# Loading and spreading V of the last two batches by halves in a tree-attention kernel

## The chip, the cores and the metric

The kernel runs on one core of one Trainium2 chip. The metric is device time in microseconds (us). A run is called fast or slow by its state: slow means over 1.5% above the fastest of the same kernel. Of the profile I use the span, from the first to the last instruction; a run's time is 1.7 to 1.9 us over its span. PE is the tensor engine. Its granted clock is in the profile too: 1.0 is full speed, and I call a stretch at 0.5 a half clock.

## The reference

Attention with a mask: query i sees key i and its ancestors in a binary tree.

```python
batch, heads, seq, dim = 8, 12, 512, 64
mask[i, i] = 1
while parent > 0: parent = (parent - 1) // 2; mask[i, parent] = 1
scores = einsum('bhqd,bhkd->bhqk', Q, K) / sqrt(dim) + (1 - mask) * (-1e9)
weights = exp(scores - max) / (sum + 1e-10)
out = einsum('bhqk,bhkd->bhqd', weights, V)
```

## The kernel before

The 96 heads are 48 pairs. GpSimd issues all loads, as float32 cast to bfloat16, in the order of `plan`; at most eight are in flight, as each later issue waits for the landing of the eighth load before it. Outputs leave through SyncE. The parts that matter are the order of the loads, the copies that spread V into the layouts v1 and vx (ten per spread, on the vector engine), and the loop.

```python
for b in range(1, B):                      # (at, tensor, batch, first head, last head + 1)
    at = HP * b - 2
    plan += [(at, Q, b, 0, 4), (at, K, b, 0, 4),
             (at + 2, Q, b, 4, 8), (at + 2, K, b, 4, 8)]
    if b < B - 1:
        plan += [(at + 3, V, b + 1, 0, H), (at + 4, Q, b, 8, H), (at + 4, K, b, 8, H)]
    else:
        plan += [(at + 4, Q, b, 8, 10), (at + 4, K, b, 8, 10),
                 (at + 5, Q, b, 10, H), (at + 5, K, b, 10, H)]
# ... cut ...
for i in range(N):                         # N = 48 pairs, HP = 6 pairs a batch
    b, hp = pairs[i]
    load(i + 9)
    if i + 2 < N:
        transposes(i + 2)                  # PE, then qt (vector engine) and kt (scalar engine)
    if i + 1 < N:
        scores(i + 1)                      # PE, then two exp on the scalar engine
    values(i)                              # PE, then rec and of on the vector engine, output DMA
    # ... cut: batch 0 ...
    elif b + 1 < B and hp:
        if hp == 1:
            todo = spread(b + 1, 0, H)     # ten copies, for all 12 heads
        copies(todo[2 * hp - 2:2 * hp])    # two in each of five steps
```

All PSUM tiles, which take what PE puts out, have one buffer.

The softmax here doesn't subtract the row's maximum and nothing guards it: scores larger than these inputs give would overflow.

Of the kernel before, what the change touches and what calls it, by code (L numbers as in the profile page):

```python
# [126 lines left out]
def kernel(  # L127
# [8 lines left out]
    B, H, S, D = Q.shape  # L136
# [3 lines left out]
    HP = H // 2  # L140
# [11 lines left out]
    for t in range(T):  # L152
        o = sorted(range(T), key=lambda r: KCOL[t, r])
        at = [KCOL[t, r] for r in o]
# [32 lines left out]
    for i in range(NV):  # L187
# [9 lines left out]
    psumO = ctx.enter_context(tc.tile_pool(name="psumO", bufs=1, space=PSUM))  # L197


    plan = [(0, Q, 0, 0, 2), (0, K, 0, 0, 2), (0, V, 0, 0, 6), (0, Q, 0, 2, 6),  # L200
            (0, K, 0, 2, 6), (0, V, 0, 6, H), (1, Q, 0, 6, 10), (1, K, 0, 6, 10),
            (3, Q, 0, 10, H), (3, K, 0, 10, H), (3, V, 1, 0, H)]
    for b in range(1, B):
        at = HP * b - 2
        plan += [(at, Q, b, 0, 4), (at, K, b, 0, 4),
                 (at + 2, Q, b, 4, 8), (at + 2, K, b, 4, 8)]
        if b < B - 1:
            plan += [(at + 3, V, b + 1, 0, H), (at + 4, Q, b, 8, H),
                     (at + 4, K, b, 8, H)]
        else:  # L210
            plan += [(at + 4, Q, b, 8, 10), (at + 4, K, b, 8, 10),
                     (at + 5, Q, b, 10, H), (at + 5, K, b, 10, H)]
    plan.reverse()
    loaded = {}

    def load(upto):
        while plan and plan[-1][0] <= upto:
            _, src, b, h0, h1 = plan.pop()
            kind = "q" if src is Q else "k" if src is K else "v"
            if (kind, b) not in loaded:  # L220
                loaded[kind, b] = stage.tile([P, H, T * D], bf16, name=kind + "s")
            nc.gpsimd.dma_start(  # L222
                out=loaded[kind, b][:, h0:h1, :],
                in_=src[b, h0:h1].rearrange("h (p t) d -> p h (t d)", t=T),
            )

    def pick(v, t0, t1):

        stop = t1 + (1 if t1 > t0 else -1)
        return v[:, :, t0:stop if stop >= 0 else None:t1 - t0, :]  # L230

    def spread(b, h0, h1):
        vs = loaded["v", b]
        v1, vx = v1s[b % NV], vxs[b % NV]
        v = vs[:, h0:h1, :].rearrange("p h (t d) -> p h t d", t=T)
        big = [
            (vx[64:P, h0:h1, 0:3:2, 0:D], v[64:P, :, 0:3:2, :]),
            (vx[0:64, h0:h1, 1:4:2, 0:D], v[64:P, :, 1:4:2, :]),
        ]
        for part, c, t0, t1 in ((0, 0, 1, 2), (32, 0, 3, 0), (64, 1, 2, 1),  # L240
                                (96, 1, 0, 3)):
            assert KORD[XW[c] + part // 32] == (t0, 1)
            assert KORD[XW[c + 2] + part // 32] == (t1, 1)
            big.append((
                vx[part:part + 32, h0:h1, c:c + 3:2, 0:D],
                pick(v[32:64], t0, t1),
            ))
        small = [
            (v1[32 * r:32 * r + 32, h0:h1, 0:D], v[0:32, :, KORD[K1 + r][0], :])
            for r in range(T)  # L250
        ]
        ops = []
        for n in range(6):
            ops.append(big[n])
            if n % 3:
                ops.append(small.pop())
        return ops

    def copies(ops):
        for o, i in ops:  # L260
            nc.vector.tensor_copy(out=o, in_=i)  # L261

    pairs = [(b, hp) for b in range(B) for hp in range(HP)]
    N = len(pairs)
    state = {}

    def transposes(i):
        b, hp = pairs[i]
        qs, ks = loaded["q", b], loaded["k", b]
        tq = psumT.tile([P, 512], bf16)  # L270
        tk = psumT.tile([P, 576], bf16)

        def put(o, src, t, mat):
            for hi in range(2):
                nc.tensor.matmul(  # L275
                    out=o[D * hi:D * hi + D], rhs=perms[mat],
                    lhsT=src[:, 2 * hp + hi, D * t:D * t + D],
                    start=True, stop=True, is_transpose=True,
                )

        put(tq[:, 64:192], qs, 0, 1)
        put(tq[:, 0:384].rearrange("d (c x) -> d c x", c=2)[:, :, 0:64], qs, 1, 0)
        for t in range(2, T):
            put(tq[:, P * t:P * t + P], qs, t, 0)
        for t in range(T):
            at = kput[t][1]
            if at[1] - at[0] == 32:
                step, run = at[2] - at[0], 64
            else:
                step, run = at[1] - at[0], 32  # L290
                assert at[2] - at[1] == step
            o = tk[:, at[0]:]
            o = bass.AP(o.tensor, o.offset, [list(o.ap[0]), [step, P // run], [1, run]])
            put(o, ks, t, 2 + t)
        qt = work.tile([P, 512], bf16)
        kt = work.tile([P, 512], bf16)
        nc.vector.tensor_copy(out=qt[:, :], in_=tq[:, :])  # L297
        nc.scalar.copy(  # L298
            out=kt[:, :].rearrange("d (i j x) -> d i j x", j=2, x=32),
            in_=tk[:, :].rearrange("d (j i x) -> d i j x", j=2, x=32)[:, 0:8],  # L300
        )
        state[i] = (qt, kt)
# [39 lines left out]
    def values(i):  # L342
        b, hp = pairs[i]
        v1, vx = v1s[b % NV], vxs[b % NV]
        et1, etx = state.pop(i)
        o2 = psumO.tile([P, 2, 512], fp32)
        for hi, order in ((0, (0, 1)), (1, (0, 1)), (0, (2, 3)), (1, (2, 3))):
            h = 2 * hp + hi
            for t in order:
                for kind in range(2):  # L350
                    parts = ((0, P, t),) if t >= 2 else (
                        (0, 64, 1 - t), (64, P, t))
                    for p0, p1, c in parts:
                        if kind == 0:
                            e, v = et1[:, hi, P * c + p0:P * c + p1], v1[:, h, 0:D + 1]
                        else:
                            e, v = etx[:, hi, c, p0:p1], vx[:, h, c, 0:D + 1]
                        nc.tensor.matmul(  # L358
                            out=o2[p0:p1, hi, (D + 1) * t:(D + 1) * (t + 1)],
                            lhsT=e, rhs=v, start=kind == 0, stop=kind == 1,  # L360
                        )
        o4 = o2[:, :, 0:T * (D + 1)].rearrange("p h (t x) -> p h t x", t=T)
        rec = opool.tile([P, 2, T, 1], fp32)
        nc.vector.reciprocal(out=rec[:, :, :, :], in_=o4[:, :, :, D:D + 1])  # L364
        of = opool.tile([P, 2, T * D], fp32)
        of4 = of[:, :, :].rearrange("p h (t d) -> p h t d", t=T)
        nc.vector.tensor_tensor(  # L367
            out=of4, in0=o4[:, :, :, 0:D],
            in1=rec[:, :, :, :].to_broadcast([P, 2, T, D]), op=ALU.mult,
        )  # L370
        nc.sync.dma_start(
            out=out[b, 2 * hp:2 * hp + 2].rearrange(
                "h (p t) d -> p h (t d)", t=T
            ),
            in_=of[:, :, :],
        )

    E = mybir.EngineType
    with tc.manual_schedule(engines={E.PE, E.DVE, E.Activation, E.Pool}):
        load(3)  # L380
        transposes(0)
        scores(0)
        transposes(1)
        copies(spread(0, 0, 6))
        for i in range(N):
            b, hp = pairs[i]
            load(i + 9)
            if i + 2 < N:
                transposes(i + 2)
            if i + 1 < N:  # L390
                scores(i + 1)
            values(i)
            if b == 0:
                if hp in (0, 3):
                    todo = spread(0, 6, H) if hp == 0 else spread(1, 0, H)
                cuts = (0, 3, 6, 10)
                copies(todo[cuts[hp % 3]:cuts[hp % 3 + 1]])
            elif b + 1 < B and hp:
                if hp == 1:
                    todo = spread(b + 1, 0, H)  # L400
                copies(todo[2 * hp - 2:2 * hp])


# [28 lines left out]
```

## Time and profile before

| | before |
|---|---|
| time, median (4 runs) | 156.95 us (156.81 to 157.46) |
| profiled execution | 157.8 us, span 156.0 us |
| last load lands | 137.8 us |
| out(38), out(40), out(47) | 131.5, 137.1, 152.7 us |
| vector engine, scalar engine, PE busy | 66%, 71%, 77% of the span |

I call out(i) the start of the output DMA of pair i, which waits for the last vector instruction of that pair; the differences of these times are the lengths of the steps. From the summary of waits of the kernel before (who waits for whom: us in total, times, the longest):

```profile
PE o L358 <- DVE v L261: 4.8, 8, 1.5
```

The values of the first pair of a batch (and of pair 3 in batch 0, whose V comes by halves) wait for the last copy of their V.

### The profile page before, as it was taken

How to read it: one execution, taken by the hardware profiler on the slowest of the kernel's cores; microseconds unless marked ns; L12 is line 12 of the kernel's file. 1: busy time of each engine (PE TensorE's matmuls, PEld its weight loads, DVE VectorE, ACT ScalarE, POOL GpSimd, SP SyncE). 2: the span in 40 equal slices, each digit the busy share in tenths (PEclk: the TensorE clock that was granted, in tenths of full speed). 3: DMA queues.
4: the chain of work that ended last, by engine and by line, in shares of the span. 5: the costliest groups of instructions: out<-in, count | busy, mean ns of one | idle time of the engine just before them, and what ended most of it. 6: DMA issues, size and time to landing. Idle time of an engine off the chain costs nothing.

```text
span 156.0 us, 5918 instructions
## 1 busy us (share of the span) xinstructions
PE 120.0 (77%) x2592; PEld 86.2 (55%) x2592; DVE 102.8 (66%) x243; ACT 111.0 (71%) x145; POOL 48.8 (31%) x65
## 2 busy tenths in 40 slices
PE   0539983966989897786998949986998659989950
PEld 0226752644667675564676627664676426767740
DVE  2119798097499876975589664986699635696541
ACT  3145792565799996985598937996899816999950
POOL 7974712333441323403432143503341130000000
PEclk9999999597799999999699977999999965999996
DMA  4999999999999999999999999999999999933432
GB/s 139 154 187 196 193 215 239 226 200 220 219 226 240 235 233 241 225 237 227 222 221 237 234 235 226 215 236 238 227 227 235 243 227 215 211 113 132 138 113 93
DMA packets 51210, 32.33 MB, mean 207 GB/s; under 512 B 1776, under 2 KB 51056, under 8 KB 51184
## 3 DMA queue, kind: packets, MB, share of 16 engines
q0 software_dynamic: 37840, 18.88, 89.6%
q1 hardware_dynamic: 13344, 13.08, 29.3%
q8 instruction: 20, 0.33, 0.8%
q14 instruction: 6, 0.05, 0.1%
HBM read 38.24 MB, written 12.58 MB: 326 GB/s over the span
## 4 chain that ended last, share of the span: by engine, by line
DMA 78%; PE 8%; DVE 4%; issue 3%; ACT 3%; POOL 2%; POOLq 0%
DMA ks<-in_K_dram 40%; DMA qs<-in_Q_dram 23%; DMA vs<-in_V_dram 15%; PE o L358 3%; DVE of L367 2%; PE st L311 2%; ACT etx L335 2%; PE stx L311 1%; POOL qs L222 1%; PE tk L275 1%; ACT kt L298 1%; PE tq L275 1%; DVE vx L261 1%; DVE rec L364 1%; ACT et L324 1%
## 5 line engine op out<-in xcount | busy, mean ns | idle before, releaser
L298 ACT COPY kt<-tk 128x512 bf16<-128x512 bf16 x48 | 28.2, 587 | 34.5 <-PE tk L275 33.9
L324 ACT ACTIVATE et<-st 128x1024 bf16<-128x1024 f32 x48 | 49.2, 1024 | 4.0 <-PE st L311 3.5
L358 PE MATMUL o<-v,et 128*64 128x65 bf16 (+1 forms) x576 | 39.0, 204 | 6.1 <-DVE v L261 4.8
L335 ACT ACTIVATE etx<-stx 128x768 bf16<-128x768 f32 x48 | 38.6, 804 | 0.0
L358 PE MATMUL o<-vx,etx 128*64 128x65 bf16 (+1 forms) x576 | 37.8, 200 | 0.8 <-issue 0.8
L358 PEld LDWEIGHTS <-et 128*64 128x64 bf16 (+1 forms) x576 | 28.9, 110 | 13.6 <-DVE v L261 5.9
L367 DVE TENSOR_TENSOR of<-o,rec 128x512 f32<-128x512 f32 x48 | 33.2, 691 | 1.7
L275 PE MATMUL tq<-ptile,qs 128*64 128x128 bf16 x384 | 21.6, 237 | 15.6 <-DMA qs<-in_Q_dram 10.1
L364 DVE RECIPROCAL rec<-o 128x8 f32<-128x8 f32 x48 | 9.8, 205 | 35.7 <-PE o L358 35.5
L222 POOL DMA_DIRECT2D qs<-in_Q_dram x26 | 20.3, 780 | 41.8 <-DMA vs<-in_V_dram 25.9
L358 PEld LDWEIGHTS <-etx 128*64 128x64 bf16 (+1 forms) x576 | 30.0, 111 | 0.4 <-issue 0.4
L261 DVE COPY vx<-vs 32x1536 bf16<-32x1536 bf16 (+3 forms) x54 | 28.8, 533 | 1.2
L222 POOL DMA_DIRECT2D ks<-in_K_dram x26 | 19.5, 750 | 30.7 <-DMA qs<-in_Q_dram 20.4
L275 PE MATMUL tk<-ptile,ks 128*64 128x128 bf16 x384 | 21.6, 238 | 8.4 <-DMA ks<-in_K_dram 8.1
L297 DVE COPY qt<-tq 128x512 bf16<-128x512 bf16 x48 | 19.9, 414 | 9.8 <-PE tq L275 9.3
L311 PEld LDWEIGHTS <-kt 64*128 64x128 bf16 x480 | 19.9, 102 | 11.4 <-issue 4.2
L275 PEld LDWEIGHTS <-qs 128*64 128x64 bf16 x384 | 15.2, 116 | 17.3 <-DMA qs<-in_Q_dram 10.6
L275 PEld LDWEIGHTS <-ks 128*64 128x64 bf16 x384 | 15.6, 121 | 10.7 <-DMA ks<-in_K_dram 9.4
L311 PE MATMUL st<-ctile 64*128 64x512 bf16 x96 | 20.3, 419 | 0.1
L311 PE MATMUL st<-qt,kt 64*128 64x512 bf16 x96 | 20.2, 417 | 0.1
L311 PE MATMUL stx<-qt,kt 64*128 64x96 bf16 x384 | 17.7, 215 | 0.5 <-issue 0.5
L311 PE MATMUL stx<-ctile 64*128 64x384 bf16 x96 | 17.3, 356 | 0.1
(11 smaller groups left out, 35.7 us busy)
## 6 DMA issues: line engine op xcount, KB each, us to landing
out_dram<-of SPq DMA_DIRECT2D x48, 256.0 KB, 6.2
qs<-in_Q_dram POOLq DMA_DIRECT2D x22, 256.0 KB, 19.1
ks<-in_K_dram POOLq DMA_DIRECT2D x22, 256.0 KB, 18.7
vs<-in_V_dram POOLq DMA_DIRECT2D x7, 768.0 KB, 22.4
vs<-in_V_dram POOLq DMA_DIRECT2D x2, 384.0 KB, 7.3
qs<-in_Q_dram POOLq DMA_DIRECT2D x4, 128.0 KB, 10.4
ks<-in_K_dram POOLq DMA_DIRECT2D x4, 128.0 KB, 10.0
ctile<-tree_codes SPq DMA_DIRECT2D x1, 288.0 KB, 3.1
```

Of the source, the lines that this page charges most:

```text
L222: nc.gpsimd.dma_start(out=loaded[kind, b][:, h0:h1, :], in_=src[b, h0:h1].rearrange("h (p t) d -> p h (t d)", t=T),)
L261: nc.vector.tensor_copy(out=o, in_=i)
L275: nc.tensor.matmul(out=o[D * hi:D * hi + D], rhs=perms[mat], lhsT=src[:, 2 * hp + hi, D * t:D * t + D], start=True, stop=True, is_transpos ...
L297: nc.vector.tensor_copy(out=qt[:, :], in_=tq[:, :])
L298: nc.scalar.copy(out=kt[:, :].rearrange("d (i j x) -> d i j x", j=2, x=32), in_=tk[:, :].rearrange("d (j i x) -> d i j x", j=2, x=32)[:, 0:8],
L311: nc.tensor.matmul(out=dst, lhsT=lhsT, rhs=rhs, start=first, stop=True, skip_group_check=not first,)
L324: nc.scalar.activation(out=et1[:, :, :], in_=st1[:, :, :], func=AF.Exp, scale=scale)
L335: nc.scalar.activation(out=etx[:, :, :, 32:P], in_=stx[:, :, 0:384].rearrange("p h (c q) -> p h c q", c=T), func=AF.Exp, scale=scale,)
L358: nc.tensor.matmul(out=o2[p0:p1, hi, (D + 1) * t:(D + 1) * (t + 1)], lhsT=e, rhs=v, start=kind == 0, stop=kind == 1,)
L364: nc.vector.reciprocal(out=rec[:, :, :, :], in_=o4[:, :, :, D:D + 1])
L367: nc.vector.tensor_tensor(out=of4, in0=o4[:, :, :, 0:D], in1=rec[:, :, :, :].to_broadcast([P, 2, T, D]), op=ALU.mult,)
```

## The change

V of batches 6 and 7 is loaded by halves of six heads, each just ahead of the Q and K that go with it, instead of whole half a batch earlier. Thus the loads that are needed last are not held up by V of pairs that come later. Each half is spread in the two steps before its first use. The last pair's transposes go behind the values of two pairs before, so that late Q and K would not block PE. The first loads take four heads instead of two.

```diff
-    plan = [(0, Q, 0, 0, 2), (0, K, 0, 0, 2), (0, V, 0, 0, 6), (0, Q, 0, 2, 6),
+    plan = [(0, Q, 0, 0, 4), (0, K, 0, 0, 4), (0, V, 0, 0, 6), (0, Q, 0, 4, 8),
 ... cut ...
+    for b in range(whole, B):              # whole = B - 2
+        at = HP * b - 2
+        for h0 in (0, 6):
+            plan.append((at - 1, V, b, h0, h0 + 6))
+            cuts = (6, 8, 10, H) if b == B - 1 and h0 else (h0, h0 + 6)
+            for n, (g0, g1) in enumerate(zip(cuts, cuts[1:])):
+                plan += [(at + n, x, b, g0, g1) for x in (Q, K)]
+            at += 3
 ... cut ...
-            if i + 2 < N:
+            if i + 3 < N:
                 transposes(i + 2)
             if i + 1 < N:
                 scores(i + 1)
             values(i)
+            if i + 3 == N:
+                transposes(i + 2)
 ... cut ...
+            elif HP * whole <= i - i % 3 + 3 < N and i % 3:
+                if i % 3 == 1:
+                    nb, nh = pairs[i + 2]
+                    todo = spread(nb, 2 * nh, 2 * nh + 6)
+                copies(todo[5 * (i % 3) - 5:5 * (i % 3)])
```

More of the change, by code (lines that the diff above doesn't have):

```diff
@@ L197 @@
     psumO = ctx.enter_context(tc.tile_pool(name="psumO", bufs=1, space=PSUM))
-    plan = [(0, Q, 0, 0, 2), (0, K, 0, 0, 2), (0, V, 0, 0, 6), (0, Q, 0, 2, 6),
-            (0, K, 0, 2, 6), (0, V, 0, 6, H), (1, Q, 0, 6, 10), (1, K, 0, 6, 10),
-            (3, Q, 0, 10, H), (3, K, 0, 10, H), (3, V, 1, 0, H)]
-    for b in range(1, B):
-        at = HP * b - 2
-        plan += [(at, Q, b, 0, 4), (at, K, b, 0, 4),
-                 (at + 2, Q, b, 4, 8), (at + 2, K, b, 4, 8)]
-        if b < B - 1:
-            plan += [(at + 3, V, b + 1, 0, H), (at + 4, Q, b, 8, H),
-                     (at + 4, K, b, 8, H)]
-        else:
-            plan += [(at + 4, Q, b, 8, 10), (at + 4, K, b, 8, 10),
-                     (at + 5, Q, b, 10, H), (at + 5, K, b, 10, H)]
+    plan = [(0, Q, 0, 0, 4), (0, K, 0, 0, 4), (0, V, 0, 0, 6), (0, Q, 0, 4, 8),
+            (0, K, 0, 4, 8), (0, V, 0, 6, H), (2, Q, 0, 8, H), (2, K, 0, 8, H),
+            (3, V, 1, 0, H)]
+    whole = B - 2
+    for b in range(1, whole):
+        at = HP * b - 2
+        for n in range(3):
+            plan += [(at + 2 * n, x, b, 4 * n, 4 * n + 4) for x in (Q, K)]
+            if n == 1 and b + 1 < whole:
+                plan.append((at + 3, V, b + 1, 0, H))
+    for b in range(whole, B):
[6 more added lines that the diff above has]
+            at += 3
     plan.reverse()
@@ L397 @@
                 copies(todo[cuts[hp % 3]:cuts[hp % 3 + 1]])
-            elif b + 1 < B and hp:
+            elif b + 1 < whole:
                 if hp == 1:
                     todo = spread(b + 1, 0, H)
-                copies(todo[2 * hp - 2:2 * hp])
+                if hp:
+                    copies(todo[2 * hp - 2:2 * hp])
+            elif HP * whole <= i - i % 3 + 3 < N and i % 3:
[3 more added lines that the diff above has]
+                copies(todo[5 * (i % 3) - 5:5 * (i % 3)])
 _INS = ['Q', 'K', 'V']
```

## The prediction

> **What bounds the kernel now.** Names first. A step i of the loop transposes Q and K of head pair i+2, computes scores of pair i+1 and values of pair i; there are 48 steps, and the vector engine gives each step qt (0.41 us), rec, of, and copies that spread V. I call out(i) the end of of(i). One load of one head of one tensor is a unit (128 rows of 1 KB); the stream has 288 of them.
>
> I read the page's slices first, to see which resource is full at which time.
>
> ```profile
> PE   0539983966989897786998949986998659989950
> DMA  4999999999999999999999999999999999933432
> ...
> HBM read 38.24 MB, written 12.58 MB: 326 GB/s over the span
> ```
>
> A digit is a fortieth of 156.0 us, or 3.9 us. The DMA row is full from slice 2 to slice 35 (136.5 us) and then nearly idle, while PE still works. So there are two stages: transfers set the pace up to some 137 us, and compute alone sets the last 18 us. The chain of waits says when the hand-over happens, and what follows:
>
> ```profile
> 107.56 19.55 DMA ks<-in_K_dram
> 127.12 0.04 issue
> 127.16 0.64 PE tk L275 x8
> ...
> 138.76 0.69 DVE of L367
> 139.46 0.03 issue
> 139.49 0.55 DVE vx L261
> 140.05 0.36 DVE v L261
> 140.41 0.04 issue
> 140.46 0.79 PE o L358 x23
> ```
>
> Up to 127.1 us the chain is loads. K of batch 6, heads 8 to 11, lands at 127.12 and lets step 38 begin; from there it is compute to the end, 28.9 us for ten steps. The second part shows the thing that I think decides this case: values(42), the first pair of batch 7, start 0.05 us after the last vector copy of V. From the vector engine's timeline, out(40) to out(47) are at 137.07, 139.48, 142.25, 144.41, 146.56, 148.73, 150.78 and 152.69 us (starts of the output DMAs, which wait for of). A step without copies takes 2.16, bound by the scalar engine, whose three instructions of a step run without a gap there. The step that waits for copies takes 2.77. The kernel ends 3.35 us after out(47).
>
> The copies' cost by size:
>
> ```profile
> L261 DVE COPY vx<-vs 32x1536 bf16<-32x1536 bf16 x28 | 16.4, 585 | 0.6
> L261 DVE COPY v<-vs 32x768 bf16<-32x768 bf16 x28 | 11.0, 392 | 0.6
> ...
> L261 DVE COPY vx<-vs 32x768 bf16<-32x768 bf16 x8 | 2.9, 365 | 0.1
> L261 DVE COPY v<-vs 32x384 bf16<-32x384 bf16 x8 | 2.4, 304 | 0.1
> ```
>
> The first two rows spread 12 heads, the last two 6. Half the heads cost 62% and 78% of the time.
>
> **What the Trainium skill says.** "DMA: Bandwidth & Descriptors", Where 436 GB/s comes from, gives about 358 GB/s of HBM for each core. The trace agrees: from the landings of the loads that end batches 1 to 6 (39.00, 56.15, 74.30, 92.28, 109.48, 127.12 us) a batch takes 17.6 us for 36 units and 6 outputs, 4.72 + 1.57 = 6.29 MB, which is 357 GB/s. So no order of loads moves more bytes in that stage. The same page, Queues, rings and completion order, says that an engine alternates between its rings; loads and outputs then share the rate, and the trace has outputs landing in about 6.2 us beside loads and 2.1 without. "TensorE: Matmul & The Clock Gate", Part 1, says that the clock halves after a window of 3413 ns with too little PE work. In this trace the granted clock is 0.5 in stretches of 3.41 or 6.83 us, each after a window with PE busy 0.53 or less; windows of 0.68 kept it at 1. The same page, Architectural detail, says that the vector engine's queue is strictly first in, first out; so whatever stands behind the copies waits for all of them, as values(42) show.
>
> **The change part by part.**
> Transfers. Without outputs the stream took 8.82 us for 26 units (8.94 to 17.76 us), 0.339 us a unit; a batch then leaves (17.6 - 36 x 0.339)/6 = 0.90 us an output. The total is not changed. The order is: V of batch 6 moves from before the last K of batch 5 to behind it, and V of batch 7 from before the last Q, K of batch 6 to two halves inside batch 7. The units that stand before step 34 fall from 236 to 234; step 38 needs 252 instead of 264, and step 40 needs 270 instead of 272. The first loads of four heads let out(0) come 2 or 3 us earlier (K lands about 1.3 us later, but pair 1 does not wait for 11.6 us). As the stage after is bound by bytes, that is not seen at the end. I set it at 0.
>
> Anchor: before, unit 208 landed at 99.36 with about 26.5 outputs done. After, K of batch 6, heads 0 to 5 (unit 234), lands at 99.36 + 26 x 0.339 + 5.3 x 0.90 = 112.9; steps 32 and 33 no longer starve (before, 3.7 us from out(31) to out(32)), and no copies stand in steps 30 to 33, so out(33) is near 112.5. Step 34 then starts at 112.9 and out(34) comes 2.9 us later (transposes of K, scores 0.87, values 0.73, rec and of 0.95), at 115.8.
>
> The copies. In a block of three steps (34 to 36, 37 to 39, 40 to 42, 43 to 45) ten half copies stand in two steps, five each: 3 x 0.365 + 2 x 0.26 (their warm length in the timeline) + gaps = 1.67 us, against 0.92 for the two full copies of a step before. First step to second: the vector engine does copies 1.67, qt 0.42, rec and of 0.96, together 3.05. Second to third: values of the next half's first pair wait for the last copy, so 1.67 + 0.79 for the values + 1.01 for rec and of = 3.47. Third to first: 2.2, PE and the scalar engine as before. A block is 8.7 us, and its transfers, 18 x 0.339 + 3 x 0.90, are 8.8: about level. So out(37) is 124.8, out(40) 133.7 (K of batch 7, heads 0 to 5, unit 270, near 130.8), 3.4 us ahead of before.
>
> The tail. Before, out(40) to out(47) took 15.6. After: out(43) +8.7, out(44) +3.05, out(45) +3.47, then out(47) +4.4. The last pair was 3.96; its transposes now follow values(45), so kt (0.59) and qt come after the other exp, and the scalar engine waits for the scores, 0.4 or so. Sum 19.6. Its K, unit 288, lands near 142, while step 45 starts at about 146, so the move protects from nothing. Out(47) = 133.7 + 19.6 = 153.3; end 156.7, against 156.04. The gain of 3.4 us from the loads is more than eaten by 4.0 us of copies and order. The timed runs are 0.94 us over the profiled span (156.98 against 156.04), which gives 157.6.
>
> **Rivals.**
> (a) The copies hide. If PE and the scalar engine were far enough ahead for the steps to stay at 15.6 us, the end is 133.7 + 15.6 + 3.35 = 152.7, or 153.6 timed, 2.2% faster. For it: the intent, and the vector engine is only 66% busy. Against: values(42) waiting in the trace of before with even 0.92 us of copies, and no spare buffer for o, tq or st (one of each).
> (b) The clock drops. The two waits of PE in a block (about 0.8 and 1.15 us, 3.4 us from the first's start to the second's end) can fall in one window and leave it near 0.45 busy. Each such window costs about 1.1 us (a step took 3.3 at half clock, 2.2 at full). Two of them in the tail make 159.8. Against: the window runs freely, and it needs to line up; I give one block a chance of a quarter.
> (c) Transfers are the bound to the end: unit 288 at about 142 plus 9 us of one pair's work is 151 in span. Against: steps 42 to 47 still need some 20 us after unit 270.
>
> **Range and chances.** The sum is 157.6. A smaller effect of the copies pulls down by up to 4, cold windows push up by 1 to 2. The range is 154.6 to 160.8. Faster by over 2% means under 153.84, which is rival (a) in full: 0.12. Slower by over 2%, over 160.12, needs (b) twice or more: 0.13. Within: 0.75.
>
> **What would show it.** Right: no DMA wait over 2 us after 110 us; out(40) near 133.7; the waits of the values for the vector copies near 1 us at steps 36, 39, 42 and 45; steps of 3.0 and 3.5 us in each block; a chain that ends in DVE copies and PE o. Wrong: steps 34 to 45 at 2.2 to 2.4 us with copies in them (rival a), a granted clock of 0.5 between 125 and 150 us (rival b), or a chain of loads until 140 us (rival c).

## The result, and the profile after

The changed kernel took 159.65 us in the median (158.89 to 161.46, 4 runs, one of them slow), against 156.95. The ratio is 1.015, with a 95% interval of 1.010 to 1.020: slower, by less than 2%. Ratios here are the mean time of one kernel's fast runs over that of the other's in the same rounds, so they are not quite the ratio of the medians.

The slices of the changed kernel (span 157.8 us, a digit is 3.9 us):

```profile
PE   0188985958997579883998769979786969596760
PEclk9999999599999999999599968999999999999699
DMA  4999999999999999999999999999999999931222
```

The DMA row is the same as before: full to about slice 35, then nearly idle. The bytes are the same, and the loads end at 139.7 us instead of 137.8. What changed is the chain of waits (start, us, what). Before, a load stands on it up to 127.12 us. Now the last one lands at 92.24 us (K of batch 4), and from step 26 to the end the chain is compute:

```profile
72.75 19.48 DMA ks<-in_K_dram
92.24 0.04 issue
92.28 0.64 PE tk L280 x6
```

Its tail, cut to two of the places where the values wait for the copies:

```profile
138.08 0.26 DVE v L266
138.34 0.04 issue
138.39 0.79 PE o L363 x24
...
146.65 0.26 DVE v L266
146.91 0.04 issue
146.95 1.21 PE o L363 x24
148.16 0.57 PE tq L280 x7
148.72 0.45 PE tk L280 x8
```

Twice in the tail the values begin 0.05 us after the last copy of a half: at 138.39 (step 42) and 146.95 us (step 45). The second time the 24 matmuls take 1.21 us instead of 0.79, as the clock is halved. Of the chain from 133 us on, vector instructions are 48%; the tail of before has the scalar engine's exp there from 141.9 to 148.5 us.

The summary of waits, answering to the line of before:

```profile
PE o L363 <- DVE v L266: 8.4, 11, 1.8
```

The copies of the whole kernel, by form (count, then busy us and mean ns of one):

```profile
L266 DVE COPY vx<-vs 32x1536 bf16<-32x1536 bf16 x20 | 11.3, 563 | 0.4
L266 DVE COPY v<-vs 32x768 bf16<-32x768 bf16 x20 | 8.6, 432 | 0.4
L266 DVE COPY vx<-vs 32x768 bf16<-32x768 bf16 x24 | 8.6, 359 | 0.4
L266 DVE COPY v<-vs 32x384 bf16<-32x384 bf16 x24 | 6.2, 260 | 0.3
```

Of each of these two sorts eight full copies went and sixteen half copies came. In all, this is only 2.8 us more work on the vector engine in the page (102.8 to 105.6 us busy). It hurts because of where it stands.

Where the 1.7 us of span come from, in steps (rounded, so that sums can be 0.01 off):

| stretch | before | after | difference |
|---|---|---|---|
| up to out(40) | 137.07 | 133.76 | -3.31 |
| out(40) to out(45) | 11.66 | 15.40 | +3.74 |
| out(45) to out(47) | 3.96 | 5.24 | +1.28 |
| out(47) to the end | 3.35 | 3.37 | +0.02 |
| span | 156.04 | 157.76 | +1.72 |

In these two executions out(40) came 3.3 us earlier with the new order of loads, and the last seven steps gave back 5.0 us. The 3.3 is the difference of two single executions: over all profiles, out(40) lies at 134.28 to 137.07 us in the four that load batches 1 to 7 in the old order (before and three experiments), and at 133.50 to 135.35 in the eight with the loads of the changed kernel (in one of them by two heads). The means are 2.1 us apart. In time the difference is 2.7 us and not 1.7, as the profiled execution of before was 0.9 us slower than its median, and that of the changed kernel 0.1 us faster.

### The profile page after: what moved, and what is told of

The parts are those of the page before. It is cut to its first block, busy times and chain, and to the rows that moved or that the text cites. A ratio compares the mean times of both kernels' runs of the same rounds, so it can differ in the third digit from the quotient of the medians.

```text
span 157.8 us, 5936 instructions
## 1 busy us (share of the span) xinstructions
PE 117.3 (74%) x2592; PEld 85.0 (54%) x2592; DVE 105.6 (67%) x263; ACT 110.6 (70%) x145; POOL 48.4 (31%) x63
## 4 chain that ended last, share of the span: by engine, by line
DMA 55%; DVE 20%; PE 17%; issue 4%; POOL 2%; ACT 0%; POOLq 0%
DMA ks<-in_K_dram 29%; DMA vs<-in_V_dram 14%; DMA qs<-in_Q_dram 12%; PE o L363 8%; DVE vx L266 7%; DVE of L372 6%; DVE v L266 4%; PE st L316 3%; PE stx L316 2%; PE tq L280 2%; DVE rec L369 2%; PE tk L280 2%; DVE qt L302 2%; POOL qs L227 1%; POOL vs L227 1%
## 5 line engine op out<-in xcount | busy, mean ns | idle before, releaser
L363 PE MATMUL o<-v,et 128*64 128x65 bf16 (+1 forms) x576 | 38.5, 204 | 9.5 <-DVE v L266 8.4
L266 DVE COPY vx<-vs 32x768 bf16<-32x768 bf16 (+3 forms) x66 | 29.9, 453 | 1.4
L227 POOL DMA_DIRECT2D qs<-in_Q_dram x24 | 18.5, 771 | 38.2 <-DMA vs<-in_V_dram 20.7
L227 POOL DMA_DIRECT2D ks<-in_K_dram x24 | 18.6, 773 | 32.0 <-DMA qs<-in_Q_dram 16.3
L280 PE MATMUL tk<-ptile,ks 128*64 128x128 bf16 x384 | 21.0, 233 | 7.7 <-DMA ks<-in_K_dram 7.3
L316 PEld LDWEIGHTS <-kt 64*128 64x128 bf16 x480 | 19.3, 99 | 11.4 <-issue 3.0
L316 PE MATMUL st<-qt,kt 64*128 64x512 bf16 x96 | 19.5, 403 | 0.7 <-DVE qt L302 0.5
L280 PEld LDWEIGHTS <-ks 128*64 128x64 bf16 x384 | 15.1, 119 | 9.0 <-DMA ks<-in_K_dram 9.0
L316 PE MATMUL stx<-qt,kt 64*128 64x96 bf16 x384 | 16.9, 210 | 0.0
L316 PE MATMUL stx<-ctile 64*128 64x384 bf16 x96 | 16.7, 344 | 0.0
## 6 DMA issues: line engine op xcount, KB each, us to landing
qs<-in_Q_dram POOLq DMA_DIRECT2D x3, 384.0 KB, 20.7
```

Source lines behind the costliest of these rows:

```text
L227: nc.gpsimd.dma_start(out=loaded[kind, b][:, h0:h1, :], in_=src[b, h0:h1].rearrange("h (p t) d -> p h (t d)", t=T),)
L266: nc.vector.tensor_copy(out=o, in_=i)
L280: nc.tensor.matmul(out=o[D * hi:D * hi + D], rhs=perms[mat], lhsT=src[:, 2 * hp + hi, D * t:D * t + D], start=True, stop=True, is_transpos ...
L316: nc.tensor.matmul(out=dst, lhsT=lhsT, rhs=rhs, start=first, stop=True, skip_group_check=not first,)
L363: nc.tensor.matmul(out=o2[p0:p1, hi, (D + 1) * t:(D + 1) * (t + 1)], lhsT=e, rhs=v, start=kind == 0, stop=kind == 1,)
```

## The experiments

My theory had three parts: the half copies lengthen the steps; the moved transposes cost and protect from nothing; half clock windows come on top. The rival was that the copies hide and that the order or size of the loads costs. Runs went on three chips; the median of the kernel before was 156.91, 157.37 and 157.86 us there, with single runs from 154.3 to 159.8. Times should therefore be compared through their ratio to before. The ratios need care as well: in the first call one run of before took 154.27 us, so that only 3 of its 11 runs count as fast, with a mean of 155.5 us. The ratios of that call are 0.7 to 1.0% above the ratios of the medians, which are 0.992 without the copies, 1.022 for the half copies alone, 0.994 for the copies handed out earlier and 1.016 for the pair in front.

**Without the copies** (wrong result: batches 6 and 7 use old V).

```diff
-                copies(todo[5 * (i % 3) - 5:5 * (i % 3)])
+                pass
```

> The changed kernel without any spread of V for batches 6 and 7; its result is wrong on purpose there. Theory (the ten half copies of a block are on the path, load order is a gain): steps from 40 on take 2.1 to 2.3 us, out(40) stays near 133.5 us as the loads allow no earlier, out(47) comes 15 to 16 us later, and the time is 153.5 to 154.8 us. Rival (the copies hide, and the new order or size of the loads costs the time): it stays at 158.5 to 160 us.

155.69 us, ratio 1.000 (0.990 to 1.010); the first loads, the load order and the moved transposes are still in. Out(40) was at 133.91, as in the changed kernel; out(40) to out(45) fell from 15.40 to 11.22 us. So the copies, and not the loads, made those steps long. The time is 0.9 us over my range. The profiled execution, 154.96 us, is only 0.2 over it; its out(40) to out(47), 15.92, is as forecast, with the moved transposes still keeping out(45) to out(47) at 4.71. Of the slower executions there is no trace. What held out(40) is named by the waits between 110 and 160 us:

```profile
PE tk L280 <- DMA ks<-in_K_dram: 2.2, 2, 1.4
```

Even without copies PE waited for K there, so at this point the loads and the steps with copies are about level.

**The half copies alone**, in the kernel before, with its own loads and order of transposes: `spread` for batches 6 and 7 as in the changed kernel, nothing else.

> The kernel before with its own loads, but with V of batches 6 and 7 spread by halves, five copies in each of two steps of three. Theory (the copies cost about 4 us in the tail): out(40) stays near 137 us and out(40) to out(47) grows from 15.6 to about 19.2 us, so the time is 159.5 to 161.5 us, 2 to 3% over before. Rival (the copies hide): within 0.5 us of 156.95.

160.36 us, ratio 1.031 (1.022 to 1.041). Out(40) was at 136.99 and out(40) to out(45) at 14.97, without a half clock in it, against 11.66. The theory held: the copies alone cost 3.3 us in these five steps.

**The same half copies, handed out earlier.**

```diff
-            elif HP * whole <= i - i % 3 + 3 < N and i % 3:
-                if i % 3 == 1:
-                    nb, nh = pairs[i + 2]
-                    todo = spread(nb, 2 * nh, 2 * nh + 6)
-                copies(todo[5 * (i % 3) - 5:5 * (i % 3)])
+            if HP * whole - 4 <= i < N - 4:
+                n = (i - 2) % 3
+                if n == 0:
+                    nb, nh = pairs[i + 4]
+                    late = spread(nb, 2 * nh, 2 * nh + 6)
+                cuts3 = (0, 3, 7, 10)
+                copies(late[cuts3[n]:cuts3[n + 1]])
```

> The changed kernel with the same half copies handed out 3, 4 and 3 over three steps, ending one step before the first values that read them. Theory (it is the two steps of five copies and the wait of the values behind the last that cost): blocks take about 7.5 us instead of 8.7 where loads don't hold them, no wait of values for vector copies over 0.3 us, and the time is 154.5 to 156.5 us. Rival (the number of copies, not their place, costs): 158 us or more, as the sum of the vector engine's work is the same.

156.00 us, ratio 1.004 (0.996 to 1.013). The kernel of the next experiment, with the copies in their old place, took 159.45, though it also has the last pair's transposes in front, the faster order by the traces. The work of the copies is the same and only its place differs, so the rival fell. Fewer copies a step and an earlier end came in one edit; how much each of them does was not separated. The vector engine's timeline of this run, from out(40) on (start, us):

```profile
133.96 0.25 DVE L266 COPY v<-vs 32x384 bf16<-32x384 bf16 x1
134.23 0.35 DVE L266 COPY vx<-vs 32x768 bf16<-32x768 bf16 x1
134.59 0.25 DVE L266 COPY v<-vs 32x384 bf16<-32x384 bf16 x1
134.77 0.41 DVE L302 COPY qt<-tq 128x512 bf16<-128x512 bf16 x1
135.58 0.21 DVE L369 RECIPROCAL rec<-o 128x8 f32<-128x8 f32 x1 [0.41 <-PE o L363]
```

Three copies end 0.88 us after out(40), where in the changed kernel five end after 1.63, and the vector engine now waits 0.41 us for PE. The wait of the values for the vector copies is gone from the list of this run's waits after 110 us; out(40) to out(45) is 12.03.

**The last pair's transposes put back in front**, in the changed kernel: `if i + 2 < N` again, and the two lines behind `values(i)` deleted.

> The changed kernel with one part undone: the last pair's transposes stand before the values again. Theory (the order costs, and protects from nothing, as K of the last pair landed at 139.7 us, over 6 us before it is used): the last two steps shrink from 5.2 us by 0.4 to 1.2 us, and the time is 158.4 to 159.3 us against 159.65. Rival (the move shields the scores and values from late K): the time does not fall, or rises by up to 1 us, with PE waiting for K in step 45.

159.45 us, ratio 1.023 (1.014 to 1.033). In time this can't be told from the changed kernel (1.015, and 1.030 in the repeat below); my range missed by 0.15. The profiled run was a slow one, with a half clock from 140.1 to 143.5 us. In its trace out(45) to out(47) was 3.73 us instead of 5.24, and no wait for K stood in step 45. K of the last pair had landed at 139.7 us in the changed kernel, while its transposes ran from 148.2 on.

**The same move alone in the kernel before.**

> The kernel before with only the last pair's transposes moved behind the values. Theory (they hide nothing and make the scalar engine wait): out(45) to out(47) grows from 4.0 to 4.7 us and the time by 0.5 to 1.0 us on that of before. Rival (it is neutral, or it helps as K of the last pair is late): within 0.3 us, or less.

157.81 us against 157.37, ratio 1.003 (0.993 to 1.013): unclear. The trace is clear: out(45) to out(47) 4.71 us against 3.96. It was 4.71 in all four profiles with the move and no half clock there, and 3.73 to 3.97 in the seven profiles of experiments without the move. So the move costs 0.75 us against before.

**PE kept busy through the wait of step 45** in the changed kernel: 24 transposes of a constant ahead of `values(45)`, into a tile nobody reads.

> The changed kernel with 24 transposes of a constant put in front of the values of step 45, where PE waited 1.76 us for the vector copies; nobody reads their result. Theory (the window of 3.4 us around that wait had PE busy 0.34 and the next one ran at half clock, which made the last steps about 1.2 us longer): PE runs the dummies inside its wait, no half clock between 140 and 152 us, out(45) to out(47) falls from 5.2 to 4.7 us or less, and the values after the wait take 0.8 instead of 1.2 us; 158.6 to 159.2 us. Rival (the half clock costs nothing, as other engines set these steps): 159.5 us or more.

159.59 us, ratio 1.019 (1.012 to 1.026): the time did not fall visibly, and lies in the rival's range. In the profile the theory's steps are seen. The windows of the changed kernel (from:to, length, busy us and count of PE, weight load, vector, scalar and GpSimd, then granted clock, DMA share, GB/s):

```profile
143.00:147.00 4.00, 1.66 (x34) 0.99 (x29) 3.71 (x12) 2.99 (x4) 0.00 (x0) 0.99 0.37 131
147.00:150.00 3.00, 2.86 (x44) 1.99 (x46) 1.23 (x3) 0.58 (x1) 0.00 (x0) 0.50 0.02 5
```

and of this run:

```profile
143.00:147.00 4.00, 3.42 (x72) 2.67 (x68) 3.81 (x12) 3.31 (x5) 0.00 (x0) 1.00 0.27 97
147.00:150.00 3.00, 2.22 (x51) 1.56 (x51) 1.58 (x5) 0.74 (x2) 0.00 (x0) 1.00 0.15 52
```

PE busy went from 1.66 to 3.42 us in the first, and the clock of the second from 0.50 to 1.00; the values after the wait took 0.80 us instead of 1.21, and out(45) to out(47) 4.71 instead of 5.24. Together 0.9 us in this execution. Other executions can have their half clock elsewhere in the tail, as the run before this one shows; why the median stays is not settled.

**The first loads alone**: the kernel before with the changed kernel's loads of batch 0.

> The kernel before with only its first loads changed to four heads. Theory (the stage after the start is bound by bytes, so the start is not seen at the end): within 0.5% of before. Rival (the start costs: in the changed kernel the second K chunk landed at 13.05 us where the kernel before had it at 11.61, and out(0) came 0.4 us later): 0.3 to 1% slower.

156.76 us, ratio 1.000 (0.993 to 1.007). The start is not seen at the end of the run.

**The changed kernel again**, on the third chip.

> The changed kernel as it is, again on another chip, as the kernel before varied from 154.3 to 159.8 us in the experiments' rounds. Expected: 159 to 160 us, 1.2 to 2.5% over the fast runs of before; out(40) near 133.8 us, out(40) to out(47) of 19.4 to 20.7 us depending on where a half clock window falls. If it were equal to before, the first comparison was chance.

161.80 us, ratio 1.030 (1.022 to 1.039). The first comparison was not chance, but the time is 1.8 us over what I expected, and the intervals of the two comparisons (1.010 to 1.020 in the first) do not meet: that the changed kernel is slower is shown, by how much only as 1 to 4%. Out(40) was 133.50 and out(40) to out(45) 15.39, as in the first profile; out(45) to out(47) was 6.39, as the half clock began at 146.4 and lasted to the end. So out(40) to out(47) was 21.78, over my 19.4 to 20.7. The wait of PE before values(45) was 1.76 us in both profiles.

**Copies early and the pair first.**

> The kernel with copies handed out early over three steps (median 156.0 us) with, in addition, the last pair's transposes before the values again. Theory (the moved transposes cost about 1 us at full clock: out(45) to out(47) was 4.7 us with them moved and 3.7 without, in the runs so far): 154.6 to 155.4 us, out(45) to out(47) 3.7 us. Rival (the move is free once the copies are out of the way): 155.7 to 156.4 us.

155.35 us against 157.37, ratio 0.990 (0.984 to 0.996); out(45) to out(47) was 3.97, where I had forecast 3.7. It beats both kernels. Against the kernel with the moved pair it is on another chip, so the gain of the order alone rests on the steps of the traces.

**The same with Q and K of the last two batches by two heads**: `cuts = range(h0, h0 + 7, 2)`.

> The kernel of copies early and pair first with Q and K of the last two batches loaded by two heads, V still by six. Theory (up to step 40 the landing of a whole chunk of three pairs sets the time, as out(40) stays near 133.8 us even without copies): step 40 needs only the first pair of its chunk, 8 units less, so out(40) moves to 130.5 to 132.5 us and the time to 151.5 to 153.8 us. Rival (smaller loads move fewer bytes per us, or the compute of the stage is the bound): out(40) stays within 1 us of 133.8 and the time within 1 us of the kernel without this edit.

155.02 us, ratio 0.987 (0.980 to 0.994), the best ratio of all, and not separated from the run above. My theory failed here: K of pair 42 landed at 126.14 us, yet out(40) was at 133.52. The chain of the changed kernel could have told me: its last load lands at 92.24 us. Here too the list of PE's waits after 93 us has no load; it is led by

```profile
PE tq L280 <- DVE qt L302: 3.2, 7, 0.7
```

So once the loads come early enough, the rival is right, and in this stretch the steps themselves are the bound: what is left to gain there lies in making them shorter.

**Another way to the same end**: the kernel before, with heads 8 and 9 of Q and K of batch 6 loaded ahead of V of batch 7, V whole and two full copies a step as ever.

```diff
+            cut = 10 if b == B - 2 else 8
+            plan += [(at + 3, x, b, 8, cut) for x in (Q, K) if cut > 8]
-            plan += [(at + 3, V, b + 1, 0, H), (at + 4, Q, b, 8, H),
-                     (at + 4, K, b, 8, H)]
+            plan += [(at + 3, V, b + 1, 0, H), (at + 4, Q, b, cut, H),
+                     (at + 4, K, b, cut, H)]
```

> The kernel before with one edit: Q and K of batch 6, heads 8 and 9, are loaded ahead of V of batch 7 instead of behind it. V is still loaded and spread whole, two full copies a step. Theory (what the changed kernel gained is that step 38 no longer starves behind V of batch 7; what it lost is the half copies): out(38) moves from about 131 us to 127 or 128 us, no copies of more than 0.9 us a step, and the time falls by 2 to 4 us to 153 to 155 us. Rival (something else holds the steps before 38 by then): within 1 us of before.

156.65 us against 157.86, ratio 0.996 (0.990 to 1.003): same as before. Out(38) was at 130.63, not 127 to 128. In the chain of this run PE stands still in the middle of values(38), for nothing that the profile shows:

```profile
127.22 0.37 PE o L360 x14
127.59 1.50 issue
129.09 0.56 PE o L360 x9
```

A 16 KB packet of the instruction queue ran from 126.8 to 127.8 us. That PE waited for its instructions is my guess; no run tests it. (The changed kernel has the like: such a packet from 111.0 to 112.0 us, and PE standing still from 112.40 to 113.44 for nothing that the profile shows.) The stall accounts for 1.5 us of the miss, the rest stays open.

**The same for batches 1 to 6.**

> The same as the run before it, for every batch from 1 to 6: heads 8 and 9 of Q and K ahead of the next V. Theory (the stage up to step 38 is bound by bytes, so fewer stalls there bring nothing but fewer half clock windows): equal to the run with the one edit within 1 us. Rival (the stalls of the earlier batches cost too): 1 us or more under it.

155.98 us, ratio 0.995 (0.989 to 1.001), within 1 us of the run above, as the theory has it.

## Why the prediction was right or wrong

The time, 159.65 us, lies in the range of 154.6 to 160.8, and "within 2%" was given 0.75. The centre, 157.6, was 2 us too low: it forecast 0.6 us over before, and 2.7 were measured. Its signs for being right were seen (after 108 us PE waited for no load), and so was one for being wrong, a half clock between 125 and 150 us. Point by point:

- **Transfers.** The landings were near: K of batch 6 (heads 0 to 5) was predicted at 112.9 and landed at 112.2; K of batch 7 (heads 0 to 5) near 130.8, and landed at 129.5. So were the steps: out(34) 115.8 and 116.53; out(37) 124.8 and 125.2; out(40) 133.7 and 133.76. But the path was not the predicted one. The prediction let K start step 34 and stand 2.9 us before out(40). In the trace PE turned to the transposes of step 34 at 112.04, just before K landed, and to those of step 40 at 130.60, 1.1 us after it: the steps set the pace there and not the loads. Out(34) came late by 0.7 us although K was early by as much, as PE stood still for the 1.04 us mentioned above; two blocks of 8.7 and 8.6 us, predicted as 9.0 and 8.9, made up for it. That out(40) was met to 0.1 us is thus luck; that loads and steps are about level is what the prediction had said and the run without copies shows. Two of its sums do not close either: 115.8 + 8.7 is 124.5, not 124.8, and two blocks of 8.8 after 112.9 end at 130.5, not 130.8.
- **The rate of the loads.** The prediction took 357 GB/s as agreeing with the limit of about 358 that it cites, and concluded that no order moves more. Its own 26 units in 8.82 us, with no output beside them, are 386 GB/s. So 358 was no limit in this trace; 357 is what this mix of loads and outputs reached. Nothing else in the sum rests on it.
- **The start.** "Out(0) come 2 or 3 us earlier" was wrong: it was at 17.77 us, against 17.35. Step 0 needs pair 2, and its K now comes in a chunk that landed at 13.05 instead of 11.61. That it is not seen at the end held.
- **The copies.** Right in mechanism and size. The block's steps were predicted as 3.05, 3.47 and 2.2 us; steps 41 to 43 took 2.96, 3.46 and 2.16. The values waited for the copies 1.05, 0.97, 0.97 and 1.76 us at steps 36, 39, 42 and 45, near 1 us as forecast but for the last. Out(40) to out(45) was predicted as 15.2 and was 14.97 without a half clock in the run of the half copies alone, and 14.98 in the changed kernel with the dummies. Running the changed kernel without them, and with them elsewhere, shows the same cause.
- **The order of the last pair.** Right in direction, too small: 4.4 us predicted, 4.71 measured at full clock.
- **The clock.** The sum had none in it; it was only rival (b). The trace has one half clock window in the tail, worth 0.95 us: 0.42 in the values of step 45 and 0.53 behind. I had looked for it in the two waits of a block. It came from the wait in front of values(45), 1.76 us long. There PE no longer had the last pair's transposes to do; with these in front, PE had two waits of 0.97 us there, 1.5 us apart, and no half clock followed. So the two late edits add up: the copies make PE wait, and the moved transposes leave that wait empty. The first half is shown by the runs; that the empty wait caused the half clock is supported by the run with dummies.
- **From span to time.** The term of 0.94 us was mis-sized. I took the median time of before less the span of its profile, but that profile was of a slower execution, 157.8 us. Time less span of the same run is 1.76 before and 1.77 after. This is 0.8 us of the miss; order and clock are most of the rest.
- **Rival (a)**, the copies hide, fell. **Rival (c)**, loads bind to the end, fell: the last load landed 18 us before the end.

## What to carry to other kernels

Splitting late data to arrive just in time also moves the work on that data just ahead of its use; check that the engine which does it has room there, and spread it over more steps, ending a step early (here both were done at once). Halving an instruction did not halve its time: here 65 to 70% of it stayed, by the distance of starts. A time that is met to a tenth can still have another cause than the forecast one: follow the chain back to its last load. An instruction moved out of the way of a wait should have a wait to avoid: look up when its data land first. And take time and span from the same run.

## What the Trainium skill lacked or had wrong

- "TensorE: Matmul & The Clock Gate", Part 1, says that the clock halves after an idle window of about 3.4 us, and that short idles between groups of matmuls can make it swing too, but not how much idle it takes. Here windows that were partly busy did it. In the profiles of before and after, from 17 to 147 us, ten windows at full clock had PE busy 0.20 to 0.56, and nine of them were followed by half clock (the exception had 0.54); none at full clock with 0.60 or more was. All 14 profiles say the same, on a grid of 3.41 us laid through the starts of half clock: of 471 full-clock windows, all 37 that were under 0.495 busy were followed by half clock, 11 of the 23 from there to 0.575, and none of the 411 above. The page has no such threshold. In the window before the half clock of the tail PE was idle for 2.27 us, 1.76 of them in one wait. To leave half clock took more: of 63 windows at half clock, the 13 under 0.85 busy were all followed by another one, of the 46 over 0.875 none; the repeat of the changed kernel had 0.87 from 146.4 us on, and stayed.
- "Perfetto Trace Analysis", Optimizing Scalar/DVE Operations, puts the fixed cost of a vector instruction on SBUF at about 60 ns. Back to back copies here start 0.56 us apart with 1536 elements and 0.365 us with 768, and 0.37 and 0.26 us with 768 and 384 for the other sort. A straight line through each pair leaves about 0.17 and 0.15 us fixed (two sizes each, so the line itself is not tested). The point is against this passage alone, as other pages of the skill have other figures.
- No page says how much a load stream delays outputs: the outputs landed in some 6.3 us beside it and in 2.07 us after it.
